# Sixteen rows of one early tile moved from SyncE's queue to GpSimd's, and the bias parts moved from GpSimd to VectorE

## The chip, the cores and the metric

The kernel runs on one core of one Trainium2 chip. The metric is device microseconds of the program, from the times of repeated runs; before the change the median of two runs is 322.68 us (322.56 and 322.79). One further execution was profiled, and all rows below come from it.

## What is computed

```python
x_heads = x.reshape(B, S, H, Dh).transpose(0, 2, 1, 3)      # B=8, S=2048, H=8, Dh=256
x_heads = x_heads + bias[None, :, None, :]
x_tiled = np.repeat(x_heads, 2, axis=2)
mx = x_tiled.max(axis=-1, keepdims=True)
lse = mx.squeeze(-1) + np.log(np.exp(x_tiled - mx).sum(axis=-1))   # float32, (8, 8, 4096)
```

The input `x` is 8 x 2048 x 2048 float32, 134 MB, and is read once. For each row and each of its eight heads of 256 elements the kernel forms the logarithm of the sum of exponentials of `x + bias`; each result is written twice.

## The kernel before

The 16,384 rows of `x` are cut into 64 tiles. A tile is 128 partitions by `K = 2` rows of 2048 float32, 2 MB; in the early tiles a partition's two rows lie side by side in memory, so that one partition's share is one piece of 16 KB, which the trace counts as one packet. Tiles live in a ring of eight buffers (`NBUF = 8`, four blocks `xbs` of two tiles each).

SyncE issues all loads of `x`. Tiles 0 and 1 are loaded one by one (`load`, `load_part`, L243), tiles 2 to 41 in pairs of 4 MB (L228), tiles 42 to 56 one by one, tiles 57 to 60 in single rows, and the last three tiles in thirteen pieces in a written order (`load_tail`). The first eight tiles are loaded at the start. A later load goes into a buffer that is used again; it is issued by `reload` and waits until the last readers of that buffer are done, VectorE's sum at L519 among them. Behind each of the first fifteen pair loads that are issued so, `mark` (L265) loads n rows of a few bytes into a scratch tile `gap`, with n = 1, 2, ... 15.

A DMA's rows are spread over 16 DMA engines. A load of 128 rows gives eight to each. The bias comes in over ScalarE's queue (`brow`, L296).

The work on most tiles (stage `BULK`) is split by heads. TensorE adds the bias to heads 0 to 2 by putting the bias into PSUM (L386) and adding `x` through an identity matrix (L444); ScalarE takes the exponential from PSUM (L455, L462). GpSimd adds the bias to heads 4 to 7 in place (`g_add`, L494); ScalarE takes the exponential of heads 3 to 7 (L500). Head 3 gets its bias as a factor on VectorE (L512), and VectorE sums (L519). The last tiles are worked row by row, and the end follows a list written out by hand (`TAIL`). The program order of every engine is that of the source (`manual_schedule`).

The start is the part that the change touches. In the order of the source:

- ScalarE issues the load of `brow`; SyncE issues tiles 0 to 7.
- VectorE sets three constants; GpSimd makes the identity matrix `ident` and a bfloat16 copy `ident_bf`. TensorE needs `ident` for every L444.
- GpSimd splits 768 biases into three bfloat16 parts `bparts` that sum to the float32 value (L309 to L313: copy, subtract, copy, subtract, copy). TensorE uses `bparts` directly for the first two tiles; ScalarE's queue spreads them to `b3` (L314) for the others.
- TensorE spreads the bias over all partitions (L319), in two halves, each copied by VectorE into `b_rep` (L325), which GpSimd's L494 needs; the second half's L319 waits for the first half's copy.
- Then the tiles begin; GpSimd's first L494 stands behind its five instructions on the bias.

Of the kernel before, what the change touches and what calls it, by code (L numbers as in the profile page):

```python
# [48 lines left out]
]  # L49

T_TAIL = 61


TAIL_LOADS = [
# [38 lines left out]
def kernel(  # L93
# [6 lines left out]
    nc = tc.nc  # L100
    P = nc.NUM_PARTITIONS
# [28 lines left out]
    bparts = sb.tile([1, 3, CPE], BF16, name="bparts")  # L130
    brest = sb.tile([1, 2, CPE], F32, name="brest")
# [3 lines left out]
    NR = KB * H * NB  # L135
    SEEN = (T_TAIL - (B - 1) * NBLK) * K
    LATE = NBLK * K - SEEN
# [29 lines left out]
    gap = sb.tile([P, 304], F32, name="gap")  # L167
    xbs = [sb.tile([P, KB, D], F32, name=f"xb{i}") for i in range(NBUF // TB)]
    xts = [xb[:, k : k + K] for xb in xbs for k in range(0, KB, K)]
# [8 lines left out]
    def modes_of(t):  # L178
        return [modes for t0, modes in STAGES if t0 <= t][-1]

    def pieces(t):

        if len(modes_of(t)) == 1:
            return [(0, K, 0, D)]
        return [(k, k + 1, 0, D) for k in range(K)]

    def rows_of(t, n=1):


        b, at = divmod(t, NBLK)  # L190
        if b < B - 2:
            blk, i = divmod(at, TB)
            v = x[b, blk * P * KB : (blk + 1) * P * KB, :]
            return v.rearrange("(p k) d -> p k d", k=KB)[:, i * K : (i + n) * K]
        v = x[b, at * P * K : (at + 1) * P * K, :]
        if b == B - 2:
            return v.rearrange("(p k) d -> p k d", k=K)
        return v.rearrange("(k p) d -> p k d", k=K)
# [5 lines left out]
    def on_x(t, ins, after):  # L204
        buf = users[t // TB % len(xbs)]
        for t_u, u in buf:
            same = u.ins.engine == ins.ins.engine
            if u not in after and (not same or t_u % NBUF == t % NBUF and t_u < t):
                tc.declare_no_dep(
                    ins.ins,  # L210
                    u.ins,
                    reason="another tile, or waited for by those it waits for",
                )
        buf.append((t, ins))
        return ins

    loads = {}

    last_uses = [[] for _ in range(T)]

    def load(t):
        if TB <= t < BLOCKS:

            if t % TB == 0:
                after = [u for i in range(TB) if t >= NBUF for u in last_uses[t + i - NBUF]]
                ins = on_x(
                    t,
                    nc.sync.dma_start(  # L228
                        out=xbs[t // TB % len(xbs)], in_=rows_of(t, TB)
                    ),  # L230
                    after,
                )
                for i in range(TB):
                    loads[t + i, 0, 0] = ins
            return
        after = last_uses[t - NBUF] if t >= NBUF else []
        for k0, k1, c0, c1 in pieces(t):
            loads[t, k0, c0] = load_part(t, k0, k1, c0, c1, after)

    def load_part(t, k0, k1, c0, c1, after):  # L240
        return on_x(
            t,
            nc.sync.dma_start(  # L243
                out=xts[t % NBUF][:, k0:k1, c0:c1],
                in_=rows_of(t)[:, k0:k1, c0:c1],
            ),
            after,
        )

    def load_tail():  # L250
        for t, k, h0, h1 in TAIL_LOADS:
            ins = load_part(t, k, k + 1, h0 * Dh, h1 * Dh, last_uses[t - NBUF])
            for h in range(h0, h1):
                loads[t, k, h * Dh] = ins
# [3 lines left out]
    def mark():  # L258

        n = marked[0] + 1  # L260
        w = 4 + n
        if n > 15:
            return
        c = marked[1]
        nc.sync.dma_start(  # L265
            out=gap[0:n, c : c + w],
            in_=bass.AP(tensor=bias.tensor, offset=bias.offset, ap=[[64, n], [1, w]]),
        )
        marked[:] = [n, c + w]

    def reload(t):

        n = t + NBUF
        if n < BLOCKS:
            if n % TB == TB - 1:
                load(n - TB + 1)
                mark()
        elif n < T_TAIL:
            load(n)
        elif n == T - 1:  # L280
            load_tail()
# [5 lines left out]
    for set_idx, (_name, funcs) in enumerate(get_activation_tables(nc.m.arch).items()):  # L287
# [9 lines left out]
        out=brow.rearrange("p (h j) -> p h j", h=H), in_=bias.unsqueeze(0)  # L297
    )
    for t in range(NBUF):
        load(t)  # L300
    nc.vector.memset(ones, 1.0)
    nc.vector.memset(ones_bf, 1.0)
    nc.vector.memset(b3, 0.0)
# [2 lines left out]


    bp = brow[:, 0:CPE]
    nc.gpsimd.tensor_copy(bparts[:, 0], bp)  # L309
    nc.gpsimd.tensor_sub(brest[:, 0], bp, bparts[:, 0])  # L310
    nc.gpsimd.tensor_copy(bparts[:, 1], brest[:, 0])
    nc.gpsimd.tensor_sub(brest[:, 1], brest[:, 0], bparts[:, 1])
    nc.gpsimd.tensor_copy(bparts[:, 2], brest[:, 1])  # L313
    nc.scalar.dma_start(out=b3[0:3, :], in_=bparts)  # L314


# [6 lines left out]
    for i, c in enumerate(range(G0, D, MM)):  # L323
# [10 lines left out]
        out=b_far,  # L334
        in_=brow,
# [5 lines left out]
        out=Rx[0][0:1, 1 + widths[0] :],  # L341
# [23 lines left out]
    def on_bank(i, ins):  # L365
        for j, u in bank_users[i // 2]:
            if j != i and u.ins.engine != ins.ins.engine:
                tc.declare_no_dep(ins.ins, u.ins, reason="another bank")
        bank_users[i // 2].append((i, ins))
        return ins  # L370
# [43 lines left out]
    def add_x(m, t, k0, c0, c1, got):  # L414


        heads = []
        for ka, kb, c, w, bank, p in got:
            if not c0 <= c < c1:
                continue  # L420
            mm = nc.tensor.matmul(  # L421
                p,
                lhsT=ident,
                rhs=xts[t % NBUF][:, ka:kb, c : c + w],
                start=False,
                stop=True,
            )
            on_bank(bank, on_x(t, mm, [loads[t, k0, c0]]))
            for i in range(0, (kb - ka) * w, Dh):
                k, cw = divmod(i, w)  # L430
                heads.append((ka + k, (c + cw) // Dh, bank, p[:, i : i + Dh], mm))
        return heads
# [6 lines left out]
    def late_heads(m, t, got, sums):  # L439


        mms = []
        for h, p in enumerate(got[:-1]):
            mm = nc.tensor.matmul(  # L444
                p,
                lhsT=ident,
                rhs=xts[t % NBUF][:, :, h * Dh : (h + 1) * Dh],
                start=False,
                stop=True,
            )  # L450
            mms.append(on_x(t, mm, [loads[t, 0, 0]]))

        def pe_part():
            for k in range(K):
                act = nc.scalar.activation(  # L455
                    out=xts[t % NBUF][:, k, 0:Dh],
                    in_=got[0][:, k * Dh : (k + 1) * Dh],
                    func=ACT.Exp,
                    accum_out=sums[:, k, 0:1],
                )  # L460
                last_uses[t].append(on_x(t, act, [mms[0]]))
            act = nc.scalar.activation(  # L462
                out=xts[t % NBUF][:, :, Dh : m["pe"] * Dh].rearrange(
                    "p k (h j) -> p h k j", j=Dh
                ),
                in_=got[-1].rearrange("p (h k j) -> p h k j", k=K, j=Dh),
                func=ACT.Exp,
            )
            on_x(t, act, [mms[-1]])

        return pe_part
# [11 lines left out]
    def each_row(src, c, n, k_rows):  # L483

        return bass.AP(
            tensor=src.tensor,
            offset=src.offset + c,
            ap=[src.ap[0], [0, k_rows], [1, n]],
        )

    def g_add(m, t, k0, k1):
        c = m["g0"] * Dh
        v = xts[t % NBUF][:, k0:k1, c:D]
        add = nc.gpsimd.tensor_tensor(  # L494
            out=v, in0=v, in1=each_row(b_rep, c - G0, D - c, k1 - k0), op=ALU.add
        )
        return on_x(t, add, [loads[t, k0, 0]])

    def exp_inplace(t, v, after):
        return on_x(t, nc.scalar.activation(out=v, in_=v, func=ACT.Exp), [after])  # L500
# [259 lines left out]
    def sums_of(t):  # L760
# [15 lines left out]
        (modes_of(t)[k0], k0, k1)  # L776
        for t in range(T_TAIL)
        for k0, k1, _, _ in pieces(t)
# [95 lines left out]

    for t in range(T_TAIL):
        if t == T_FACTORS:
# [3 lines left out]
        for k0, k1, c0, c1 in pieces(t):  # L880
            m = modes_of(t)[k0]
            add = None
            heads = []
            bias_here = bias_there
            if m["late"]:
                pe_part = late_heads(m, t, bias_here, sums)
            else:
                heads = add_x(m, t, k0, c0, c1, bias_here)

                pe_parts = [  # L890
                    lambda t=t, one=one, sums=sums: sum_biased(t, *one, sums)
                    for one in heads
                ]

                def pe_part(pe_parts=pe_parts):
                    flush(pe_parts)
# [6 lines left out]
            if m["g0"] < H:  # L903
                add = g_add(m, t, k0, k1)
# [109 lines left out]
```

## Time and profile before

| | |
|---|---|
| median of the runs | 322.68 us (322.56 to 322.79) |
| the profiled execution: its own time / its span | 323.83 / 322.0 us |
| busy PE, DVE, ACT, POOL | 246.5, 286.9, 264.4, 287.0 us |
| DMA queue of SyncE (q1) | 9024 packets, 135.15 MB, 98.2% of 16 engines' span |
| packets of 16 KB / 32 KB on that queue, median | 611 / 1213 ns |
| instruction loads of the program (q8, q14) | 5 and 9 packets, 0.08 and 0.07 MB |
| granted TensorE clock, mean | 0.951 |

The span runs from the first to the last instruction of the program. The profiled execution took 1.83 us more than its span, and 1.15 us more than the median of the runs without a profile. Besides instructions, the trace holds start, duration, size and queue of each DMA packet, and the times at which each DMA engine reported that its part of a load had landed: sixteen reports for a load of 128 rows. An instruction that issues a DMA is not counted as busy time.

### The profile page before, as it was taken

What the parts mean: (1) busy time and instruction counts of PE and PEld (TensorE: products, weight loads), DVE (VectorE), ACT (ScalarE), POOL (GpSimd) and SP (SyncE); (2) the same over time, 40 slices, a digit from 0 to 9 for tenths busy, and PEclk for the clock granted to TensorE, in tenths of its full rate; (3) what the DMA queues carried; (4) which work ended last, traced back from release to release, by engine and by line L of the source; (5) the groups of instructions that cost most, each with busy time, mean ns of one, the idle gap of its engine ahead of it and who ended that gap; (6) DMA issues with size and microseconds to landing.
All of it is one profiled execution on the core that took longest, in us unless ns stands there. A gap on an engine that the chain in (4) does not pass through costs nothing.

```text
span 322.0 us, 2284 instructions
## 1 busy us (share of the span) xinstructions
PE 246.5 (77%) x610; PEld 98.9 (31%) x610; DVE 286.9 (89%) x307; ACT 264.4 (82%) x434; POOL 287.0 (89%) x118
## 2 busy tenths in 40 slices
PE   5998885877886667868687876877787688688765
PEld 2333332323332223323233332332333233233222
DVE  1337999699989998998989999999999999989994
ACT  1159986798688888779879988889888998999994
POOL 7939997999999999999999999999999999978772
PEclk9979996899799999979989997999999999799997
DMA  7999999999999999999999999999999999999994
GB/s 300 467 407 456 415 433 450 411 440 452 407 444 452 404 438 448 411 444 437 411 453 428 423 446 411 434 430 430 426 440 428 425 430 438 417 426 426 423 413 154
DMA packets 9190, 135.45 MB, mean 421 GB/s; under 512 B 1236, under 2 KB 1623, under 8 KB 3031
## 3 DMA queue, kind: packets, MB, share of 16 engines
q1 hardware_dynamic: 9024, 135.15, 98.2%
q10 hardware_dynamic: 152, 0.14, 0.1%
q8 instruction: 5, 0.08, 0.1%
q14 instruction: 9, 0.07, 0.1%
HBM read 134.23 MB, written 1.05 MB: 420 GB/s over the span
## 4 chain that ended last, share of the span: by engine, by line
DMA 52%; POOL 18%; DVE 13%; PE 9%; ACT 7%; issue 0%; SPq 0%
DMA xb<-in_x_dram 51%; POOL xb L494 18%; DVE R L519 11%; ACT xb L500 5%; PE pair L444 3%; DVE xb L512 2%; PE one_ps L444 2%; PE pair L319 1%; PE pair L386 1%; ACT xb L462 1%; PE pair L837 1%; DMA brow<-in_bias_dram 1%; PE one_ps L386 1%; ACT xb L455 0%; ACT xb L475 0%
## 5 line engine op out<-in xcount | busy, mean ns | idle before, releaser
L494 POOL TENSOR_TENSOR xb<-xb,b_rep 128x2048 f32<-128x2048 f32 x57 | 257.6, 4544 | 19.3 <-DMA xb<-in_x_dram 19.3
L519 DVE TENSOR_REDUCE R<-xb 128x14 f32<-128x3584 f32 (+1 forms) x57 | 216.8, 3803 | 2.7 <-ACT xb L500 0.9
L500 ACT ACTIVATE xb<-xb 128x2560 f32<-128x2560 f32 (+5 forms) x78 | 155.8, 2008 | 19.0 <-POOL xb L494 18.8
L444 PE MATMUL pair<-xb,ident 128*128 128x512 f32 x216 | 109.2, 631 | 0.0
L444 PE MATMUL one_ps<-xb,ident 128*128 128x512 f32 x108 | 62.5, 663 | 17.9 <-DMA xb<-in_x_dram 17.9
L462 ACT ACTIVATE xb<-pair 128x1024 f32<-128x1024 f32 x54 | 55.5, 1028 | 17.4 <-PE pair L444 17.4
L444 PEld LDWEIGHTS pair<-xb,ident 128*128 128x128 f32 x216 | 44.4, 205 | 58.0 <-issue 58.0
L512 DVE TENSOR_TENSOR xb<-xb,w_ps 128x512 f32<-128x512 f32 x54 | 36.7, 680 | 21.2 <-ACT xb L500 21.2
L386 PE MATMUL one_ps<-b,ones_bf 128*128 128x512 bf16 x52 | 19.6, 377 | 39.5 <-ACT xb L455 39.5
L455 ACT ACTIVATE xb<-one_ps 128x256 f32<-128x256 f32 x108 | 39.9, 377 | 7.1 <-PE one_ps L444 7.1
L386 PEld LDWEIGHTS <-ones_bf 128*128 128x128 bf16 (+1 forms) x174 | 17.3, 100 | 87.1 <-issue 79.9
L386 PE MATMUL pair<-b,ones_bf 128*128 128x512 bf16 x104 | 30.8, 378 | 0.0
L444 PEld LDWEIGHTS one_ps<-xb,ident 128*128 128x128 f32 x108 | 19.7, 200 | 32.9 <-DMA xb<-in_x_dram 27.0
L535 DVE CUSTOM_DVE_ANT_0 xb<-xb,w_ps 128x256 f32<-128x256 f32 x61 | 22.2, 414 | 0.1
L455 ACT ACTIVATION_READ_ACCUMULATOR xb<-one_ps 128x1 f32 x108 | 21.9, 203 | 0.0
L421 PE MATMUL pair<-xb,ident 128*128 128x512 f32 x28 | 16.6, 699 | 6.6 <-DMA xb<-in_x_dram 6.6
L558 POOL TENSOR_TENSOR xb<-xb 128x128 f32<-128x128 f32 (+3 forms) x39 | 14.9, 383 | 4.8 <-ACT xb L848 2.0
L475 ACT ACTIVATE xb<-pair 128x256 f32<-128x256 f32 x37 | 14.1, 400 | 1.3 <-PE pair L837 1.0
L837 PE MATMUL pair<-xb,ident 128*128 128x512 f32 (+1 forms) x18 | 9.5, 613 | 3.4 <-DMA xb<-in_x_dram 3.4
L552 POOL TENSOR_TENSOR xb<-xb,w_sb 128x256 f32<-128x256 f32 (+1 forms) x10 | 7.8, 784 | 3.1 <-ACT xb L500 2.4
L421 PEld LDWEIGHTS pair<-xb,ident 128*128 128x128 f32 x28 | 4.9, 205 | 14.7 <-DMA xb<-in_x_dram 12.7
L475 ACT ACTIVATION_READ_ACCUMULATOR xb<-pair 128x1 f32 x37 | 8.3, 225 | 0.0
(61 smaller groups left out, 84.0 us busy)
## 6 DMA issues: line engine op xcount, KB each, us to landing
xb<-in_x_dram SPq DMA_DIRECT2D x20, 4096.0 KB, 22.5
xb<-in_x_dram SPq DMA_DIRECT2D x17, 2048.0 KB, 22.8
xb<-in_x_dram SPq DMA_DIRECT2D x10, 1024.0 KB, 19.7
xb<-in_x_dram SPq DMA_DIRECT2D x2, 640.0 KB
xb<-in_x_dram SPq DMA_DIRECT2D x4, 256.0 KB, 8.7
xb<-in_x_dram SPq DMA_DIRECT2D x1, 768.0 KB
xb<-in_x_dram SPq DMA_DIRECT2D x2, 384.0 KB, 12.3
out_dram<-res SPq DMA_DIRECT2D x1, 512.0 KB
```

The costliest lines, as they stand in the source:

```text
L386: nc.tensor.matmul(p, lhsT=lhsT, rhs=each_row(b, h * Dh, Dh, K), start=i == 0, stop=False,)
L421: mm = nc.tensor.matmul(p, lhsT=ident, rhs=xts[t % NBUF][:, ka:kb, c : c + w], start=False, stop=True,)
L444: mm = nc.tensor.matmul(p, lhsT=ident, rhs=xts[t % NBUF][:, :, h * Dh : (h + 1) * Dh], start=False, stop=True,)
L455: act = nc.scalar.activation(out=xts[t % NBUF][:, k, 0:Dh], in_=got[0][:, k * Dh : (k + 1) * Dh], func=ACT.Exp, accum_out=sums[:, k, 0:1],)
L462: act = nc.scalar.activation(out=xts[t % NBUF][:, :, Dh : m["pe"] * Dh].rearrange("p k (h j) -> p h k j", j=Dh), in_=got[-1].rearrange("p ...
L475: act = nc.scalar.activation(out=xts[t % NBUF][:, k, h * Dh : (h + 1) * Dh], in_=p, func=ACT.Exp, accum_out=sums[:, k, h : h + 1],)
L494: add = nc.gpsimd.tensor_tensor(out=v, in0=v, in1=each_row(b_rep, c - G0, D - c, k1 - k0), op=ALU.add)
L500: return on_x(t, nc.scalar.activation(out=v, in_=v, func=ACT.Exp), [after])
L512: mul = nc.vector.tensor_tensor(out=f, in0=f, in1=each_row(w_ps, m["pe"] * Dh - W0, n, k1 - k0), op=ALU.mult,)
L519: red = nc.vector.tensor_reduce(out=sums[:, k0:k1, h0:H], in_=v.rearrange("p k (h j) -> p k h j", j=Dh), op=ALU.add, axis=mybir.AxisListTy ...
L535: ttr = nc.vector.tensor_tensor_reduce(out=v, in0=v, in1=w, scale=1.0, scalar=0.0, op0=ALU.mult, op1=ALU.add, accum_out=dst,)
L558: done = nc.gpsimd.tensor_tensor(out=v[:, :, 0:n], in0=v[:, :, 0:n], in1=v[:, :, n : 2 * n], op=ALU.add)
```

## The change

Tile 1's load on SyncE's queue takes 112 of the 128 partitions. The other 16 are loaded by `load_shares`, a list of thirteen DMAs that GpSimd issues: they follow the list `SHARES`, where a pair `(n, real)` is n rows: rows of the tile if `real` is not zero, otherwise rows of four bias elements that go into the scratch tile `gap`. Six DMAs carry 2, 4, 2, 2, 4 and 2 rows of the tile; the seven tiny ones carry 7, 1, 1, 6, 1, 1 and 15 rows. Counted on from engine 0 with one engine a row, modulo 16, the real rows fall on engines 7, 8, 10 to 13, 15 and 0, two on each.

These thirteen DMAs stand ahead of the identity matrix in GpSimd's program. The five instructions on the bias parts move from GpSimd to VectorE, ahead of the copies into `b_rep`. All that reads tile 1 waits for seven loads where it waited for one.

```diff
+SPARED = 1
+MAIN = 112
+SHARES = [(7, 0), (2, 2), (1, 0), (4, 4), (1, 0), (2, 2), (6, 0), (2, 2), (1, 0), (4, 4), (1, 0), (2, 2), (15, 0)]
...
+    def loads_of(t, k, c):
+        ins = loads[t, k, c]
+        return ins if isinstance(ins, list) else [ins]
...
         after = last_uses[t - NBUF] if t >= NBUF else []
+        if t == SPARED:
+            ins = nc.sync.dma_start(out=xts[t][0:MAIN], in_=rows_of(t)[0:MAIN])
+            loads[t, 0, 0] = [on_x(t, ins, [])]
+            return
...
+    def load_shares(t):
+        p = MAIN
+        for i, (n, real) in enumerate(SHARES):
+            if real:
+                ins = nc.gpsimd.dma_start(out=xts[t][p : p + n], in_=rows_of(t)[p : p + n])
+                loads[t, 0, 0].append(on_x(t, ins, []))
+                p += n
+            else:
+                c = 304 - 4 * (i + 1)
+                nc.gpsimd.dma_start(
+                    out=gap[0:n, c : c + 4],
+                    in_=bass.AP(tensor=bias.tensor, offset=bias.offset, ap=[[64, n], [1, 4]]),
+                )
+        assert p == P
...
     for t in range(NBUF):
         load(t)
+    load_shares(SPARED)
     nc.vector.memset(ones, 1.0)
...
     bp = brow[:, 0:CPE]
-    nc.gpsimd.tensor_copy(bparts[:, 0], bp)
-    nc.gpsimd.tensor_sub(brest[:, 0], bp, bparts[:, 0])
-    nc.gpsimd.tensor_copy(bparts[:, 1], brest[:, 0])
-    nc.gpsimd.tensor_sub(brest[:, 1], brest[:, 0], bparts[:, 1])
-    nc.gpsimd.tensor_copy(bparts[:, 2], brest[:, 1])
+    nc.vector.tensor_copy(bparts[:, 0], bp)
+    nc.vector.tensor_sub(brest[:, 0], bp, bparts[:, 0])
+    nc.vector.tensor_copy(bparts[:, 1], brest[:, 0])
+    nc.vector.tensor_sub(brest[:, 1], brest[:, 0], bparts[:, 1])
+    nc.vector.tensor_copy(bparts[:, 2], brest[:, 1])
     nc.scalar.dma_start(out=b3[0:3, :], in_=bparts)
```

In `add_x`, `late_heads` and `g_add`, `[loads[t, k0, c0]]` becomes `loads_of(t, k0, c0)`, and likewise for the other indices.

More of the change, by code (lines that the diff above doesn't have):

```diff
@@ L427, in add_x @@
             )
-            on_bank(bank, on_x(t, mm, [loads[t, k0, c0]]))
+            on_bank(bank, on_x(t, mm, loads_of(t, k0, c0)))
             for i in range(0, (kb - ka) * w, Dh):
@@ L450, in late_heads @@
             )
-            mms.append(on_x(t, mm, [loads[t, 0, 0]]))
+            mms.append(on_x(t, mm, loads_of(t, 0, 0)))
         def pe_part():
@@ L496, in g_add @@
         )
-        return on_x(t, add, [loads[t, k0, 0]])
+        return on_x(t, add, loads_of(t, k0, 0))
     def exp_inplace(t, v, after):
```

## The prediction

> **What bounds the kernel now.** I read the DMA rows of the page first, then the chain that ended last, the waits of SyncE's queue, and the timeline of the start.
>
> ```profile
> DMA  7999999999999999999999999999999999999994
> q1 hardware_dynamic: 9024, 135.15, 98.2%
> DMA 52%; POOL 18%; DVE 13%; PE 9%; ACT 7%; issue 0%; SPq 0%
> ```
>
> The sixteen DMA engines are busy from the second slice to the last but one, 98.2% with SyncE's queue alone. A 16 KB packet takes 0.61 us and eight of them a tile: 4.86 us a tile for 64 tiles is 311 us. Only the engines' common pace, or an uneven share among them, can move the end much. The chain's last pieces:
>
> ```profile
> 283.71 19.65 DMA xb<-in_x_dram
> 303.36 0.02 issue
> 303.38 10.47 DMA xb<-in_x_dram
> 313.85 0.04 issue
> 313.89 1.16 PE pair L837 x2
> ```
>
> At 313.85 TensorE still waits for a load, which counts as landed when the slowest of its sixteen engines reports. The trace's landing reports show how uneven the engines are: tile 0's sixteen come between 7.58 and 8.11 us, but those of the load that ends at 303.36 between 301.32 and 303.36.
>
> Which engines are late can be read from the tiny loads of L265: the one of n rows shows up on n engines, always on those of the one before and one new, so the order numbers them 0 to 15; each engine keeps its lag to a few ns from load to load. Lags at 274 us behind the earliest engine, in ns: engine 13: 0, 11: 114, 12: 119, 10: 163, 8: 186, 15: 267, 7: 280, 0: 308; then 4: 489, 2: 589, 3: 1075, 6: 1337, 14: 1426, 9: 1534, 5: 1746, 1: 1923. They jump, one engine at a time, by 0.52 to 1.41 us, where an instruction packet (q8 or q14) runs: at 108 us engine 3, at 118 engine 5, at 232 engine 4, at 251 engine 9. Nothing evens them out.
>
> **What the change does to the lags.** With 112 rows each engine gets seven packets of tile 1 in place of eight: -0.607 us (the interval between two packets). GpSimd's rows give two to each of 7, 8, 10, 11, 12, 13, 15, 0: +1.214, net +0.607. These are just the eight early ones. The late eight keep -0.607. The extra reports and tiny rows are priced by the bias load of L314: its three 1.5 KB packets, at 13.40 to 13.62 us on ScalarE's queue, put engines 0, 1 and 2 back by 67 ns, 61 for the packet and 6 for the report. A late engine gets three tiny rows of 9 to 12 ns and at most thirteen reports: +0.1 us. So late engines gain 0.5 and early ones lose 0.7: engine 1 goes from 1923 to 1.42 us, engine 0 from 308 to 1.02, and the latest report of each load comes 0.5 us sooner. Bounds: no gain, and 0.607.
>
> The same row prices packets that write into partitions whose `x` other engines are writing: the three went into neighbouring partitions, 0 to 2, and whichever engine had these in its share of `x`, none of the sixteen went back by more than its own packet. I take this as no cost for the shifted rows; the other bound is in the last rival.
>
> **The start.** These rows set what can be hidden:
>
> ```profile
> 2.91 0.82 POOL L309 CAST bparts<-brow 1x768 bf16<-1x768 f32 x1 [1.23 <-DMA brow<-in_bias_dram]
> ...
> 5.07 0.69 DVE L325 COPY b_rep<-pair 128x512 f32<-128x512 f32 x1 [3.53 <-PE pair L319]
> ...
> 8.10 0.81 POOL L313 CAST bparts<-brest 1x768 bf16<-1x768 f32 x1
> ...
> 8.88 8.96 POOL L494 TENSOR_TENSOR xb<-xb,b_rep 128x2048 f32<-128x2048 f32 x2
> ...
> 12.51 2.08 PE L444 MATMUL one_ps<-xb,ident 128*128 128x512 f32 x2
> ```
>
> *Bias parts.* GpSimd loses 0.82 + 1.63 + 0.81 + 1.63 + 0.81 = 5.7 us. On VectorE I price them per element: L333's reduction of 2048 on one partition takes 2.27 us, so 0.85 for each of three copies; L512's 512 take 0.68, so 1.02 for each of two subtractions: 4.6 us, from 2.9 to 7.5. Queued behind them is L325, which ran at 5.07: +2.4 us, and with it the second L319, the second L325, L386 and L444. Bounds: none (five times the 0.06 of L331) and 3.5 (GpSimd's 5.7).
>
> *GpSimd's thirteen issues.* No row shows one. SyncE's take 0.33 (0.29 to 1.30 at L265), ScalarE's 0.54 and 0.82. I take 0.8, the costliest of the plain ones: 10.4 us from 0.75 to 11.2, then the identity with its copy (0.93) to 12.1. SyncE's queue at the end also waits for the load eight issues back; if GpSimd's ninth waits so for its first, a small load under way takes 6.4 us (L314, 8.94 to 15.3), which adds 0.8. Queued behind: `ident`, then L494. L444 then starts at about 14.9, set by the bias parts and not by `ident`. Tile 0's L494 runs at 13 to 17.5; tile 1's last rows, issued at about 11, land at about 17.4, so its L494 ends near 22 and not at 17.8. ScalarE's exponential of tile 1 began only at 25.05, so this is hidden.
>
> *What hides 2.4 us.* The next thing late is the load of tiles 8 and 9 (L228), issued at 32.1 when VectorE had summed tile 1. The engines run out of the first eight tiles at 41.15, and a load's first packet came 1.05 us after its issue (0.76 to 1.81): the cover is 41.15 - 1.05 - 32.1 = 8.0 us. Later it grows, as VectorE needs 4.5 us a tile and the DMA 4.86.
>
> ```profile
> SPq L228 <- DVE R L519: 170.7, 17, 28.3
> ```
>
> So the start costs nothing. If `ident` came later than 12.5 + 8.0 = 20.5 us, each further us would be lost for good; that needs (20.5 - 0.93 - 0.75) / 13 = 1.45 us an issue. The row's upper end, 1.30, is covered.
>
> [...]
>
> **The sum.** Landing of the load that the chain waits for: 313.85 - 0.5; start 0; so the span goes from 322.0 to 321.5 and the profiled time from 323.83 to 323.3. The median of the runs lies 1.15 below the profiled time: 322.68 - 0.5 = **322.2 us**.
>
> **Rivals.**
>
> *Rows on the lowest engines, slower.* The n-row loads on SyncE's queue always took the lowest n engines, and L314's three rows on ScalarE's queue engines 0 to 2. If GpSimd's queue does the same, nothing is counted on: engines 0 and 1 get six real rows each (four loads of two, two of four), engines 2 and 3 two. Engine 1, the latest, goes by -0.607 + 6 x 0.607 + 0.1 = +3.1 us: **325.8**. It decides from the first pair of rows. For it: both queues shown do so. Against: GpSimd's is another kind of queue.
>
> [...]
>
> *The count starts elsewhere, or other engines are struck by the instruction packets.* Then the change doesn't do what it says: a late engine gets +0.607 + 0.1: **323.4**. Against: the jumps follow program points.
>
> *The 0.5 us is hidden.* From 290 to 310 us ScalarE and VectorE are full:
>
> ```profile
> 290.00:300.00 10.00, 8.22 (x23) 3.32 (x22) 10.00 (x57) 10.00 (x25) 8.45 (x19) 1.00 1.01 424
> 300.00:310.00 10.00, 7.69 (x22) 3.00 (x21) 9.99 (x61) 10.00 (x26) 6.95 (x16) 1.00 1.01 419
> ```
>
> (After the stretch and its length: PE, PEld, DVE, ACT, POOL busy, clock, DMA share, GB/s.) If their work alone sets the end: **322.7**. Against: before 276 they too waited for loads, and at 313.89 TensorE does.
>
> *GpSimd's block is long.* At 2.0 us an issue `ident` comes at 27.7: 15.2 later, 8.0 covered, 7.2 lost: 322.2 + 7.2 = **329.4**.
>
> *Foreign rows collide.* If a group of partitions takes only one engine's pace (27 GB/s, 16 KB in 0.607 us), the sixteen rows, and MAIN's rows at seven a engine, share with the owner's: a row that shares with two others takes 1.8 us. An engine with two such rows and one or two collisions in its seven ends 3 to 5 us late: about **326.5**. Against it stands L314, with only 1.5 KB a row.
>
> [...]
>
> **How the numbers follow.** Forecast 322.2: 0.45; lowest engines 0.11; wrong engines 0.14; hidden 0.13; GpSimd's block 0.09; collisions 0.08. The range leaves out the long block (0.09), the upper part of the collisions (0.05) and a gain over 1 us (0.03): 321.7 to 326.0. Two per cent, 6.5 us, is about what a measurement of this kernel can tell from no change: slower by more is most of the long block and part of the collisions, 0.12; faster by more has no mechanism, 0.01, since perfectly even engines would gain only about 1 us; within it 0.87.
>
> **What would show it.** Right: the spread of the reports near 274 us falls from 1.9 to about 1.5 us, tile 1's last rows land by 18 us, L228's first wait ends by 36 us and L494 starts near 13. Wrong: sixteen reports of tiles 2 and 3 already spread by over 2 us (lowest engines, or collisions), `ident` after 20 us or a hole in the DMA row near 42 us (long block), or the landings 0.5 us earlier and the end unmoved (hidden).

## The result, and the profile after

The changed kernel takes 334.19 us (median of two runs, 333.52 and 334.85) where the kernel before took 322.68: the ratio is 1.036, with a 95% interval of 1.027 to 1.045. It is slower by 11.5 us; 322.2 had been forecast, with 326.0 as the upper end. The profiled execution took 334.85 us at a span of 333.0.

The DMA rows of the page after:

```profile
DMA  8999959999999999999999999999999999999993
GB/s 294 243 362 419 431 256 417 414 427 437 437 433 429 426 433 428 437 433 437 438 425 429 429 439 429 421 427 437 425 432 437 422 431 435 417 427 430 420 403 123
q1 hardware_dynamic: 9008, 134.88, 96.9%
q0 software_dynamic: 416, 0.26, 0.4%
DMA 36%; DVE 27%; ACT 16%; POOL 14%; PE 5%; issue 1%; SPq 0%; POOLq 0%
```

q0 is GpSimd's queue: 416 packets, 26 on each engine, two for each of the thirteen transfers. A slice is 8.3 us. In the second and third slice the engines are as busy as ever (9 and 9) but move 243 and 362 GB/s where the kernel before moved 467 and 407. In the sixth they are half idle. After that the rate is the old one. So the whole loss lies in the first 50 us, and it has two shapes: packets that take longer, and a hole.

The start of the chain that ended last (start, length, what):

```profile
2.99 12.30 DMA xb<-in_x_dram
15.29 0.28 issue
15.57 21.05 DMA xb<-in_x_dram
36.62 0.09 issue
36.71 2.04 PE one_ps L473 x2
```

Two of GpSimd's transfers, 4 and 2 rows long, are under way for 12.3 and 21.05 us, the second issued when the first had landed. Tile 1 is complete at 36.62. The timeline of GpSimd's and TensorE's start:

```profile
1.27 0.70 POOL L272 DMA_DIRECT2D gap<-in_bias_dram  x1 [0.82 <-POOLq L1027]
...
7.25 0.52 POOL L272 DMA_DIRECT2D gap<-in_bias_dram  x1 [1.59 <-DMA gap<-in_bias_dram]
10.56 0.52 POOL L267 DMA_DIRECT2D xb<-in_x_dram  x1 [2.79 <-DMA xb<-in_x_dram]
...
15.57 0.52 POOL L267 DMA_DIRECT2D xb<-in_x_dram  x1 [3.29 <-DMA xb<-in_x_dram]
17.43 0.52 POOL L272 DMA_DIRECT2D gap<-in_bias_dram  x1 [1.35 <-DMA gap<-in_bias_dram]
18.24 0.29 POOL masks.py:199 TENSOR_SCALAR_AFFINE_SELECT ident<-ident 128x128 f32<-128x128 f32 x1
18.59 2.08 PE L473 MATMUL one_ps<-xb,ident 128*128 128x512 f32 x2 [4.57 <-POOL ident masks.py:199]
18.85 4.50 POOL L523 TENSOR_TENSOR xb<-xb,b_rep 128x2048 f32<-128x2048 f32 x1
36.71 2.04 PE L473 MATMUL one_ps<-xb,ident 128*128 128x512 f32 x2 [11.08 <-DMA xb<-in_x_dram]
```

An issue costs GpSimd 0.52 to 0.70 us. The first eight follow each other to 5.65 us. The ninth starts at 7.25, 0.28 us after the first transfer landed (6.97); the tenth, eleventh, twelfth and thirteenth start 0.28 us after the second to fifth landed (10.28, 11.48, 15.29, 17.16). So eight are outstanding at most. This is in the program: its GpSimd DMAs signal on eight semaphores in turn (99 to 106 in the trace), and the ninth waits for the semaphore of the first, the tenth for that of the second, and so on. The identity is ready only at 18.5, and the first L473 (L444 before) waits for it. The last four landings are 31.84, 33.26, 36.62 and 39.06. VectorE sums tile 1 late, and the load of tiles 8 and 9 is issued at 49.17 instead of 32.1 (SyncE's queue: total, times, longest, us):

```profile
SPq L237 <- DVE R L548: 184.0, 17, 45.3
```

Stretches of the changed kernel (the stretch, its length, PE, PEld, DVE, ACT, POOL busy, clock, DMA share, GB/s), the last one with the hole:

```profile
7.00:14.00 7.00, 6.74 (x13) 2.43 (x13) 3.24 (x6) 0.37 (x1) 1.55 (x3) 1.00 1.08 270
14.00:20.00 6.00, 1.43 (x3) 0.84 (x3) 0.00 (x0) 0.00 (x0) 2.94 (x6) 1.00 0.99 301
...
46.00:50.00 4.00, 3.51 (x11) 1.50 (x10) 3.96 (x3) 3.97 (x7) 4.00 (x1) 1.00 0.21 90
```

The first two of these stretches in the kernel before:

```profile
7.00:14.00 7.00, 7.00 (x15) 2.65 (x14) 3.03 (x5) 0.37 (x1) 6.94 (x4) 1.00 1.07 457
14.00:20.00 6.00, 6.00 (x15) 2.07 (x14) 0.00 (x0) 3.22 (x6) 3.84 (x1) 1.00 1.01 437
```

From 7 to 14 us the DMA share is the same and the rate falls from 457 to 270 GB/s: the median 16 KB packet of SyncE's queue takes 1024 ns there, not 611.

The sixteen reports of the load of tiles 6 and 7, the last that the start issues, measure both costs: before, they came between 41.5 and 42.0 us, mean 41.8; after, between 46.4 and 53.5, mean 48.0. The mean engine is 6.2 us late, the slowest 11.5, and that is about the whole loss in time: 11.5 us by the medians, 11.0 between the spans of the two profiled executions (322.0 and 333.0). The hole from 46 to 50 us belongs to the fast engines: the slowest one works on tiles 6 and 7 until 53.5, and the next load has been in its queue since 49.2. Near 274 us the reports of one load are spread over 4.0 us; before it was 1.9. For tiles 6 and 7 the spread was 7.1: the fast engines stood idle in the hole, and the slowest made up nothing.

### The profile page after: what moved, and what is told of

Its sections match the earlier page's. It is cut to its first block, busy times and chain, and to the rows that moved or that the text cites. A ratio compares the mean times of both kernels' runs of the same rounds, so it can differ in the third digit from the quotient of the medians.

```text
span 333.0 us, 2305 instructions
## 1 busy us (share of the span) xinstructions
PE 242.2 (73%) x610; PEld 97.8 (29%) x610; DVE 289.5 (87%) x312; ACT 263.5 (79%) x434; POOL 288.0 (86%) x126
## 4 chain that ended last, share of the span: by engine, by line
DMA 36%; DVE 27%; ACT 16%; POOL 14%; PE 5%; issue 1%; SPq 0%; POOLq 0%
DMA xb<-in_x_dram 36%; DVE R L548 23%; POOL xb L523 14%; ACT xb L529 10%; DVE xb L541 4%; ACT xb L504 3%; PE pair L473 2%; PE one_ps L473 1%; PE pair L450 1%; ACT xb L491 1%; ACT xb L484 1%; ACT xb L877 0%; POOL gap L272 0%; DVE R L643 0%; ACT res L623 0%
## 5 line engine op out<-in xcount | busy, mean ns | idle before, releaser
L523 POOL TENSOR_TENSOR xb<-xb,b_rep 128x2048 f32<-128x2048 f32 x57 | 257.2, 4543 | 21.5 <-DMA xb<-in_x_dram 21.5
L473 PE MATMUL pair<-xb,ident 128*128 128x512 f32 x216 | 108.0, 624 | 0.0
L473 PE MATMUL one_ps<-xb,ident 128*128 128x512 f32 x108 | 60.0, 639 | 24.4 <-DMA xb<-in_x_dram 19.9
L491 ACT ACTIVATE xb<-pair 128x1024 f32<-128x1024 f32 x54 | 55.4, 1027 | 11.7 <-PE pair L473 11.4
L541 DVE TENSOR_TENSOR xb<-xb,w_ps 128x512 f32<-128x512 f32 x54 | 36.7, 679 | 32.1 <-ACT xb L529 32.1
L473 PEld LDWEIGHTS pair<-xb,ident 128*128 128x128 f32 x216 | 43.7, 202 | 56.5 <-issue 56.5
L473 PEld LDWEIGHTS one_ps<-xb,ident 128*128 128x128 f32 x108 | 19.8, 195 | 36.9 <-DMA xb<-in_x_dram 14.2
L866 PE MATMUL pair<-xb,ident 128*128 128x512 f32 (+1 forms) x18 | 8.1, 533 | 3.4 <-DMA xb<-in_x_dram 3.3
```

What stands on the lines that cost most here:

```text
L473: mm = nc.tensor.matmul(p, lhsT=ident, rhs=xts[t % NBUF][:, :, h * Dh : (h + 1) * Dh], start=False, stop=True,)
L491: act = nc.scalar.activation(out=xts[t % NBUF][:, :, Dh : m["pe"] * Dh].rearrange("p k (h j) -> p h k j", j=Dh), in_=got[-1].rearrange("p ...
L523: add = nc.gpsimd.tensor_tensor(out=v, in0=v, in1=each_row(b_rep, c - G0, D - c, k1 - k0), op=ALU.add)
L541: mul = nc.vector.tensor_tensor(out=f, in0=f, in1=each_row(w_ps, m["pe"] * Dh - W0, n, k1 - k0), op=ALU.mult,)
```

## The experiments

The theory from this profile: every tile is spread over all sixteen DMA engines and nothing evens them out later, so the slowest engine's lag at the end of the first eight tiles is the loss. Its rivals: the bias on VectorE; GpSimd's block and the hole; the split of tile 1 into loads of fewer rows; six more rows on the lowest engines.

### The bias parts alone (e1), and thirteen tiny loads alone (e3)

e1 is the kernel before with the five bias instructions on VectorE:

```diff
-    nc.gpsimd.tensor_copy(bparts[:, 0], bp)
+    nc.vector.tensor_copy(bparts[:, 0], bp)
...
```

> Only the bias parts move to VectorE; all loads as before. Theory (two costs: rows of tile 1 that collide on their way into the partitions, some 4.9 us, and the late landing of tile 1, some 4.7 us): neither is here, so 322.7 us, within 0.5. Rival (VectorE's five instructions delay the start and that is lost): L325 2.4 us later and the end with it, 325.

Measured: 322.54 us, ratio 1.0003 (0.9993 to 1.0014). The move costs nothing.

e3 loads tile 1 whole on SyncE's queue and makes all thirteen of GpSimd's loads tiny ones:

```diff
-        if t == SPARED:
+        if t == -1:
...
-            if real:
-                ins = nc.gpsimd.dma_start(out=xts[t][p : p + n], in_=rows_of(t)[p : p + n])
...
+            c = 304 - 4 * (i + 1)
+            nc.gpsimd.dma_start(out=gap[0:n, c : c + 4], in_=...)
```

> Tile 1 is loaded whole by SyncE; GpSimd still issues thirteen loads of the same numbers of rows, all tiny and into the scratch tile; bias parts on VectorE. Theory: GpSimd is still held up (identity at 15 to 19 us), but this is within the 8 us of cover and nothing collides: 322.7 to 323.7. Rival 1 (GpSimd's hold-up is the cost): over 330. Rival 2 (packets of GpSimd's queue slow the engines by themselves): 16 KB and 32 KB packets lengthen between 7 and 20 us as in the changed kernel, and the time is near 327.

Measured: 323.31 us, ratio 1.002 (1.0009 to 1.0032). The issues end at 12.3 us (timeline of GpSimd):

```profile
1.27 4.63 POOL L267 DMA_DIRECT2D gap<-in_bias_dram  x8 [0.82 <-POOLq L1021]
7.50 0.52 POOL L267 DMA_DIRECT2D gap<-in_bias_dram  x1 [1.59 <-DMA gap<-in_bias_dram]
...
11.80 0.52 POOL L267 DMA_DIRECT2D gap<-in_bias_dram  x1 [0.70 <-DMA gap<-in_bias_dram]
12.31 0.22 POOL masks.py:197 MEMSET ident<- 128x128 f32 x1
```

So the thirteen issues, which hold GpSimd until 12.3 us here, and their rounds of reports cost 0.7 us (0.3 to 1.0 by the interval). The transfers land slowly for their size: at 7.2, 8.1, 9.1 us and so on to 27.4, the last five 1.6 to 2.4 us apart. Each transfer has two packets on each engine (416 packets for thirteen transfers on the page of the changed kernel), and a 32 KB packet of SyncE's takes 1.21 us: distances of up to 2.4 us fit one packet of SyncE's ahead of each of the two.

This run also shows the placement, since its tiny rows can be followed engine by engine: six rows went to engines 0 to 5, two to 0 and 1, four to 0 to 3, fifteen to 0 to 14. So these loads of 2, 4, 6 and 15 rows on GpSimd's queue took the lowest engines each time; nothing counts on. (The loads of one row go as four pieces of one element: the trace of the changed kernel has 28 packets of 16 bytes, for 7, 6 and 15 rows, and none for the single rows.) So the six real transfers of 2, 4, 2, 2, 4, 2 rows put six rows on each of engines 0 and 1 and two on 2 and 3. The packets of the changed kernel agree: two engines carry six 16 KB rows each, two carry two, and twelve carry none.

### The split of tile 1 (e2, e7, e11, e12)

All four keep the bias on GpSimd, drop GpSimd's loads, and load tile 1 with two DMAs of SyncE's queue. e2 cuts it at partition 112, e7 at 64:

```diff
             ins = nc.sync.dma_start(out=xts[t][0:MAIN], in_=rows_of(t)[0:MAIN])
-            loads[t, 0, 0] = [on_x(t, ins, [])]
+            rest = nc.sync.dma_start(out=xts[t][MAIN:P], in_=rows_of(t)[MAIN:P])
+            loads[t, 0, 0] = [on_x(t, ins, []), on_x(t, rest, [])]
...
-MAIN = 112
+MAIN = 64        # e7 only
```

e11 takes the even and the odd partitions, e12 all partitions and one row of the two:

```diff
+            ins = nc.sync.dma_start(out=xts[t][0:P:2], in_=rows_of(t)[0:P:2])       # e11
+            rest = nc.sync.dma_start(out=xts[t][1:P:2], in_=rows_of(t)[1:P:2])
...
+            ins = nc.sync.dma_start(out=xts[t][:, 0:1], in_=rows_of(t)[:, 0:1])     # e12
+            rest = nc.sync.dma_start(out=xts[t][:, 1:2], in_=rows_of(t)[:, 1:2])
```

> Tile 1 is loaded by SyncE alone, as 112 rows and then 16 rows; no GpSimd loads, bias parts on GpSimd as before. If the collisions come from the uneven split of the rows over the engines: 16 KB packets of tile 1 take about 1.0 us where 0.61 is usual, the first report of tiles 2 and 3 comes 2 to 4 us after 21.8, and the time is 325 to 327. Rival (GpSimd's queue itself slows the engines): packets stay at 0.61 us and the time at 322.7.

> Tile 1 is loaded by SyncE alone in two loads of 64 partitions; everything else as before the change. If engines collide because partitions belong to groups that take only one engine's pace, 64 partitions reach half the groups with all sixteen engines: 16 KB packets of about 1.2 us, up to 4.9 us lost, 325 to 327.5. Rival (the 112-row split costs for another reason, such as seven packets not filling an engine): packets stay at 0.61 us, 322.7.

> Tile 1 by two SyncE loads of 64 rows, the even partitions and the odd ones, instead of 0 to 63 and 64 to 127. Theory: what made the 64-row loads slow (327.7 us, 16 KB packets of 1.25 us) is that each load's packets go to one half of the partitions at a time; spread over all of them they take 0.61 to 0.75 us again, 322.5 to 324. Rival: any load of fewer rows than 128 is slow, whatever its partitions: 327 to 328 again, packets of 1.25 us.

> Tile 1 by two SyncE loads of all 128 partitions, half of the row's bytes each (8 KB packets). Theory: a second load and smaller packets cost nearly nothing when each load covers all partitions: 322.4 to 323.6. Rival: it is the number of transfers or reports that made the split loads slow: over 325.

Measured: e2 326.64 us, 1.0138 (1.0114 to 1.0162); e7 327.67 us, 1.0148 (1.0121 to 1.0175); e11 322.98 us, 1.0003 (0.9991 to 1.0016); e12 322.79 us, 1.0000 (0.9987 to 1.0013). The stretch from 7 to 14 us, first of e2:

```profile
7.00:14.00 7.00, 7.00 (x14) 2.54 (x14) 3.04 (x5) 0.37 (x1) 6.18 (x3) 1.00 1.11 302
```

of e7:

```profile
7.00:14.00 7.00, 7.00 (x15) 2.58 (x14) 3.03 (x5) 0.37 (x1) 5.86 (x3) 1.00 1.03 236
```

of e11:

```profile
7.00:14.00 7.00, 7.00 (x15) 2.78 (x14) 3.04 (x5) 0.37 (x1) 6.93 (x4) 1.00 1.09 466
```

and of e12:

```profile
7.00:14.00 7.00, 7.00 (x14) 2.48 (x13) 3.04 (x5) 0.37 (x1) 6.94 (x4) 1.00 1.07 457
```

Read the last column: with 64 neighbouring partitions a load the rate is half, with 64 spread ones it is whole. The median 16 KB packet takes 1253 ns in e7, 960 in e2, 611 in e11, and the 8 KB packet 309 in e12. Eight packets a tile and engine at 1.25 instead of 0.61 are 5.1 us, which is e7's loss of 5.0. So a load is slow by where its rows go in a stretch of time, and not by being one of two, by its number of rows or by small packets. And none of it is made up later: in e2 the last report is 3.9 us late for tiles 6 and 7, and as late for the last load.

Between e7 (236 GB/s) and e11 (466) only the partitions differ that the 64 rows of a load go to. Why a packet of e2, with 112 neighbouring rows and then 16, still took 0.96 us, and which packets met there, was not settled.

### Sixteen rows, evenly or not (e5, e6, e10, e9)

e5 and e6 are the changed kernel without tiny loads, with GpSimd's sixteen rows in one DMA (e5, one row for each engine) or in the six transfers (e6):

```diff
-SHARES = [(7, 0), (2, 2), (1, 0), (4, 4), (1, 0), (2, 2), (6, 0), (2, 2), (1, 0), (4, 4), (1, 0), (2, 2), (15, 0)]
+SHARES = [(2, 2), (4, 4), (2, 2), (2, 2), (4, 4), (2, 2)]          # e6
...
+        ins = nc.gpsimd.dma_start(out=xts[t][MAIN:P], in_=rows_of(t)[MAIN:P])   # e5, in place of the loop
```

> GpSimd loads the same sixteen rows in one DMA, without tiny ones; SyncE's load stays at 112 rows. Theory (three costs: the 112-row split collides, 4.0 us by the run with SyncE alone; the small transfers all sit on the lowest engines, so engines 0 and 1 get six rows each; the late landing of tile 1 empties the DMA): sixteen rows go one to an engine and land by 12 us, so only the first cost is left: 326.6, within 0.7, sixteen reports of tiles 2 and 3 within 0.7 us. Rival (GpSimd's queue itself is what costs): over 329.

> Only the six transfers with rows of tile 1, no tiny ones between them. Theory: twelve packets an engine on GpSimd's queue and not 26, so tile 1's last rows land at 18 to 24 us (36.6 in the changed kernel) and the DMA doesn't run empty near 48 us; engines 0 and 1 still get six rows each and lag by 4 to 6 us: 329 to 332. Rival 1 (the small transfers go round the engines one after the other, sixteen rows on sixteen engines): no lag, 326.6. Rival 2 (the hole is not from the late landing): still a hole, 334.

Measured: e5 327.55 us, 1.0144 (1.0122 to 1.0165), 0.25 above the upper end of what was expected; e6 334.4 us, 1.0365 (1.0321 to 1.0410), well above it and as slow as the changed kernel. Taking out the tiny loads and the last five issues gains nothing. Nor does the hole matter: in e6 tile 1's last rows land at 23.3 us, the load of tiles 8 and 9 goes out at 36.0, and the rate from 46 to 50 us is 426 GB/s. In e6's trace, which has few small packets, the engines can be followed: between 0.5 and 42 us two engines carry six real rows each, and they get 784 KB of SyncE's data; the two with two rows get 848, the twelve without a row 880, and all sixteen got 1056 in the kernel before. The two are behind the twelve by 96 KB, six rows; and the twelve are behind by 176 KB, 6.7 us at 0.607 us for 16 KB, of which one packet is the one that SyncE's queue no longer has.

In e10 and e9 tile 1 comes whole on SyncE's queue, and GpSimd loads the sixteen rows a second time into a scratch tile, in one DMA (e10) or in the six transfers among the tiny ones (e9):

```diff
-        if t == SPARED:
+        if t == -1:
...
+    twin = sb.tile([P, K, D], F32, name="twin")
...
-                ins = nc.gpsimd.dma_start(out=xts[t][p : p + n], in_=rows_of(t)[p : p + n])
-                loads[t, 0, 0].append(on_x(t, ins, []))
+                nc.gpsimd.dma_start(out=twin[p : p + n], in_=rows_of(t)[p : p + n])      # e9
...
+        nc.gpsimd.dma_start(out=twin[MAIN:P], in_=rows_of(t)[MAIN:P])                    # e10, in place of the loop
```

> Tile 1 whole by SyncE; GpSimd copies the same sixteen rows into the scratch tile in one transfer, without tiny loads: the same bytes as in the run with the six copies, one row for each engine. Theory of the slowest engine: one packet of 0.61 to 1.5 us (1.46 us was the median of such a row in the run with one sixteen-row load) on each engine: 323.3 to 324.4. Rival, bytes by GpSimd's queue are dear wherever they go: as the run with the six copies, over 326.

> Tile 1 comes whole by SyncE again; GpSimd's thirteen loads stay, but the six with real rows write copies into a scratch tile that nothing reads. What is left of the change is the extra work of the lowest engines: six more 16 KB rows on engines 0 and 1, two on 2 and 3. Theory: the slowest engine's lag sets the end, six rows by 0.61 us are 3.7 us, a little more with the tiny rows' turns: 326.3 to 327.8, tiles 6 and 7 last reported 3.7 to 5 us later than in the kernel before while their first reports hardly move. Rival: an uneven load of the engines is absorbed, and only the split of tile 1 costs: under 323.8. Rival: GpSimd's rows as such disturb every engine: all reports of tiles 6 and 7 late alike, and about 328 or more.

Measured: e10 325.43 us, 1.0079 (1.0060 to 1.0099), e9 331.31 us, 1.0269 (1.0247 to 1.0292), both above what was expected. The same bytes cost 2.65 us evenly and 8.5 unevenly. In e9 the mean report of tiles 6 and 7 is 3.3 us late, the last one 8.2. On the slower of the two engines with six copies these last 4.84 us together (0.61 each alone, 3.64), and SyncE's packets, 832 KB in 42 us, last 35.3 us where 0.607 for each 16 KB would be 31.6. So of its 8.2 us some 3.6 are the six rows, and most of the rest is packets drawn out, the copies by 1.2 us and SyncE's by 3.7. The sixteen reports of tiles 6 and 7 in e9 fall into three groups: eight between 43.4 and 43.7 us, six between 45.2 and 46.0, and two at 49.2 and 50.2. Followed by their packets, the last two are engines 0 and 1; the six are engines 2 and 3, with two copies each, and engines 12 to 15, which carry none. So GpSimd's rows do not slow all engines alike, as the last rival had it; they single out four that have no row of their own. All rows go into partitions 112 to 127. That these four engines are held up because they write the same partitions fits this, e7 and e11, but no run here shows which engine writes which partition, and rows into other partitions were not tried. In e10, where each engine has one of the sixteen rows, the median row takes 1.39 us and all engines are late alike (2.6 us in the mean, 2.8 for the last).

### No wait, or another tile (e8, e4)

e8 is the changed kernel with tiles 2 to 7 loaded one by one, so that SyncE's packets there are of 16 KB; e4 makes the change on tile 7, with tiles 6 and 7 loaded one by one:

```diff
-        if TB <= t < BLOCKS:
+        if NBUF <= t < BLOCKS:                                         # e8
...
-SPARED = 1
+SPARED = 7                                                             # e4
-        if TB <= t < BLOCKS:
+        if TB <= t < BLOCKS and t not in (SPARED - 1, SPARED):
```

> The changed kernel, with tiles 2 to 7 loaded one by one, so that SyncE's packets there are 16 KB and not 32 KB. Theory (a packet of GpSimd's queue waits out one SyncE packet on its engine): tile 1's last rows land at 20 to 26 us and not at 36.6, and the hole near 48 us goes; the collisions and the lag of engines 0 and 1 stay: 329 to 332. Rival (the landing is late for GpSimd's own reasons): 36 us and 334 as before.

> The same change on tile 7, which is wanted last of the first eight (tiles 6 and 7 are then loaded singly). Theory: the late landing, near 37 us, is now before its tile is wanted, so the hole of some 4.7 us near 46 us goes, while the collisions stay: 326 to 328. Rival (GpSimd's hold-up is the cost): unchanged at 334. If neither the collisions nor the hold-up cost anything: 322.5.

Measured: e8 334.41 us, 1.0365 (1.0336 to 1.0394); e4 339.89 us, 1.0565 (1.0519 to 1.0612). Both expectations missed. In e8 tile 1's last rows land at 30.7 and not at 36.6 us, the load of tiles 8 and 9 goes out at 43.8, and the rate from 46 to 50 us is 463 GB/s: the hole is gone and the time is the same. In e4 that load goes out at 35.1 and there is no hole either, yet the time is the worst: the last report of tile 7 comes at 58.4, 16.4 us late. So the hole and GpSimd's long landing cost nothing beyond the slowest engine's lag, which sets the time. Without a hole the spread of the reports stays, too: 6.5 us for tiles 6 and 7 in e8 and 7.3 near 285 us. Why the same transfers draw it out further in the middle of the load than at its start was not found.

### All runs by one measure

Lag of the reports of the load that brings tile 7, against the kernel before (mean 41.8, last 42.0 us), and the loss in time against the kernel before on the same chip:

| run | mean lag | slowest engine's lag | loss in time |
|---|---|---|---|
| e1 bias parts only | 0.0 | 0.0 | -0.1 |
| e12 halves of the rows | 0.0 | 0.1 | 0.0 |
| e11 even and odd partitions | 0.1 | 0.3 | 0.2 |
| e3 tiny loads only | 0.2 | 0.3 | 0.7 |
| e10 copies, even | 2.6 | 2.8 | 2.7 |
| e2 112 and 16 | 4.0 | 3.9 | 4.0 |
| e5 one load of 16 | 4.7 | 4.7 | 4.9 |
| e7 64 and 64 | 5.1 | 5.2 | 5.0 |
| e9 copies, lowest engines | 3.3 | 8.2 | 8.5 |
| e6 six real transfers | 6.7 | 9.8 | 11.8 |
| the change | 6.2 | 11.5 | 11.5 |
| e8 single tiles | 6.7 | 11.7 | 11.8 |
| e4 tile 7 | 7.6 | 16.4 | 17.3 |

The loss in time follows the slowest engine and not the mean: e9 has a smaller mean lag than e2 and twice its loss. Only e6 is off by over 1 us, and why was not found. The lags are those of one profiled execution and the losses are medians; repeated executions of the kernel before lie up to 1.4 us apart, those of e4 3.2, so no closer agreement can be asked. The change is also about the sum of its parts: e2's split (4.0) and e9's uneven rows (8.5), less the packet of tile 1 that each engine no longer has from SyncE (0.6), are 11.9 against 11.5. This is no rule: the same sum for e5, from e2 and e10 (2.7), gives 6.1 where 4.9 was measured.

## Why the prediction was wrong

- **What bounds the kernel: right.** The slowest engine's reports set the end, nothing evens the engines out, and the table shows it to within 1 us in all runs but one.
- **Which engines get the rows: the step that failed first.** The forecast took the count that the list is built on, a row for each next engine. No run shows that count, on which it rested that the late engines get none of the rows and gain 0.5 us. e3's trace shows the lowest engines each time (two rows on 0 and 1, four on 0 to 3, six on 0 to 5, fifteen on 0 to 14), and the trace of the changed kernel sixteen reports for each load whatever its rows (208 for thirteen). The first rival (0.11) had the lowest engines from the two queues that the trace of before shows. That the queue is of another kind (q0 `software_dynamic`, q1 and q10 `hardware_dynamic` on the page after) was no ground for the other reading.
- **Rows into partitions "whose `x` other engines are writing": priced at nothing, and the packets were drawn out by about 8 us.** L314's three 1.5 KB packets were taken as proof for 16 KB rows. The split of tile 1 alone drew the 16 KB packet from 0.61 to 0.96 us and cost 4.0 us; six rows on the lowest engines cost 8.5, of which 3.6 were the rows. The last rival had rows that meet on their way into the partitions (0.08, 326.5). Its assumption, a group of partitions at the pace of one engine, fits e7 against e11 (236 and 466 GB/s) and was not shown beyond them. It was right that the split costs, but it was priced as an alternative to the lowest engines when the two add up: 325.8 from the one and 4 more from the other would have been 329.8, already outside the range. The rest is the drawing out of the low engines' own packets, which no term had. That the place of the rows decides is shown for SyncE's loads (e7 against e11); for GpSimd's rows the reason stays argued.
- **The gain of 0.5 us: never to be seen.** The packet fewer is there in the sum above, as 0.6.
- **The bias parts: hidden, as forecast.** Three copies of 0.55 us and two subtractions of 0.95 us took 3.7 us, from 2.94 to 6.6; 4.6 had been forecast. e1 bears it out.
- **GpSimd's issues: the size was wrong, the outcome right.** 0.52 and not 0.8 us each, but the wait for the landing eight back, which was priced at 0.8 us for the ninth alone, held each of the last five, so that `ident` came at 18.5 and not at 12.1. That is inside the 20.5 that the cover allowed. L523, which is L494 in the kernel before, started at 18.85 and not near 13. e6, where no issue waits, is as slow as the changed kernel, and e3, with waits until 12.3, loses 0.7 us, so this is not where the loss lies.
- **Tile 1's landing: 36.6 and not 17.4 us.** The price of 6.4 us from L314 held for the first transfer (5.7); later ones took up to 21.6. The first long wait of SyncE's queue, forecast to end by 36, ended at 49, and the hole that was named as a wrong sign appeared. But it costs nothing beyond the slowest engine's lag: e6 and e8 have no hole and the same time.

## What to carry to other kernels

Where all transfers are spread over the same DMA engines, ask of a change what the slowest engine gets more, in packets and in their length; the mean rate, the bytes and a hole in the DMA row can mislead. A load that covers only some neighbouring partitions can take twice the time for its bytes (e7: 1253 ns for a 16 KB packet, not 611), so a tile that has to be cut is better cut along its free dimension (e12, 0.0 us lost) or into interleaved partitions (e11, 0.2 us), which cost nothing that could be told here. Before rows are given to chosen engines, find out with a few tiny loads which engines they go to.

## What the runs showed of the hardware

- GpSimd-issued loads of 2, 4, 6 and 15 rows put them on DMA engines 0 and 1, 0 to 3, 0 to 5 and 0 to 14, one row each (e3); thirteen such loads, of 1 to 15 rows, gave 208 reports, sixteen each (the changed kernel).
- GpSimd's loads beside SyncE's queue of 32 KB packets (1.21 us each): the last five tiny ones landed 1.6 to 2.4 us apart (e3), and a transfer of 32 KB took 21 us (the changed kernel).
- GpSimd's issue takes 0.52 to 0.70 us in the changed kernel, and an issue that waits for an earlier landing starts 0.28 us after it. (That the ninth waits for the first is the program's doing.)
- With rows into partitions 112 to 127 on the lowest engines, engines 12 to 15, which carry none of them, were late too: their reports for tiles 6 and 7 came between 45.2 and 46.0 us, those of engines 4 to 11 between 43.4 and 43.7 (e9).
- 64 neighbouring partitions a load: 236 GB/s; 64 alternating ones: 466; 112 neighbouring ones followed by 16: 302 (7 to 14 us).
